# Two changes to matmul shapes in a two-layer encoder kernel: values projected like queries and keys and then transposed, and small low-rank products over all 128 rows

## The chip, the cores and the metric

One core of one Trainium2 chip runs the whole program. The metric is device time in microseconds (us) of one execution. Several executions of a kernel are timed, and their median counts. A profile is one further execution, recorded by the hardware profiler; its span runs from the first to the last instruction.

The engines are TensorE (PE for its matmuls, PEld for its weight loads), VectorE (DVE), ScalarE (ACT), GpSimdE (POOL) and SyncE (SP, which only issues DMAs here). In a matmul one operand is stationary (it is loaded into the array first, by a weight load) and the other one is moving (its columns stream through, at most 512 of them into one PSUM bank).

## What is computed

A trunk of two layers is applied to two independent sequences of 512 tokens with 1024 channels, in float32. The kernel calls them streams 0 and 1. Layer 0 mixes with windowed attention and a long convolution, layer 1 with a recurrence (RWKV-7); a convolutional feed-forward block (FFN) stands behind each. The two places that matter here:

```
# layer 0: one projection; 3 groups of 4 heads of 64, so 256 value columns a group
proj = h @ p['w_in']
qkv = proj[..., :3 * ATTN_WIDTH].reshape(B, L, 3, N_PATTERNS, ATTN_HEADS_PER_GROUP, HEAD_DIM)
...
    o = jnp.einsum('bnhqk,bnkhd->bnqhd', p / den, vw)
# layer 1: low-rank decay (w) and rate (a), inner width 64, one pair for each direction
for direction in range(2):
    w_log = -jax.nn.softplus(-(p['w0'][direction] + jnp.tanh(xw @ p['w1'][direction]) @ p['w2'][direction])) - 0.5
    ...
    a = jax.nn.sigmoid(p['a0'][direction] + (xa @ p['a1'][direction]) @ p['a2'][direction])
```

The three attention groups look at the sequence with dilation 1, 4 and 16. The kernel handles groups 1 and 2 in the order of the four residues of the token number modulo 4.

## The kernel before

Activations lie with channels on partitions and 512 tokens along the free axis, in eight tiles of 128 channels. Every float32 number is split in two parts, high and low (`h0h`, `h0l`, ...; `whi`, `wlo`), and a product is made of three matmuls: high by high, low by high, high by low. `load_w` (line 97) fetches up to 1024 weight columns with one DMA issued by ACT, makes `whi` on ACT (line 108) and `wlo` on POOL (line 112). `dense` (line 121) is the standard projection: weights stationary, 512 tokens moving, 8 x 3 = 24 matmuls into one bank of a pool of three (tile `pd`), then a copy out of it. All matmuls are recorded at line 78, transposes (a matmul by the identity, which is moving) at line 81.

**Values in layer 0** (`project`, lines 452 to 469, the branch for `hp == 0`). Attention needs the values with tokens on partitions, so here the activations are stationary and 256 weight columns move. For each of the 3 groups and 2 streams that is 96 matmuls into two `pd` banks (named `pv`), fetched as two weight loads. `perm` picks the 128 tokens of a block: for group 0 they are adjacent, for groups 1 and 2 every fourth one, so that the stationary operand is read with a stride of four values. Then ACT copies both banks into `V` (line 469). Queries and keys of the same group (line 474) are dense projections, and ACT puts their tokens into residue order while it copies them out of PSUM.

`attend` works on a pair of heads: scores on PE (`ps<-qk,qk`), mask and maximum on DVE (lines 503 and 504, or 516 and 518), exponential on ACT (line 534), transposes of the result on PE (`ps<-ident,sb`), a copy out (lines 540 and 542), the product with `V` on PE (`ps<-pt,V`). Its score tiles are called `sb` and rotate through four buffers. Its banks come from a pool of five, shared with the modulation matmuls (`ps<-adaw,sc`) that run beside stream 0.

**Wide part of layer 1** (`rw_project`, the loop that ends the function). There are 8 rounds for each stream, one for each tile of 128 output channels. A round is a dense projection of `wv`, one product with `hselt`, then for rate (`la`) and decay (`lw`) and both directions d two matmuls: `wh` with the stacked hidden tile (rows of both parts, 128 rows), and `wl` with its high part alone, which is 64 rows: 0 to 63 for d = 0 and 64 to 127 for d = 1. The sums go through a sigmoid on ACT (line 912). Two 128-row products and one 96-row product for the gate (`lg1ah`, `lg1al`, `lg1b`) and four transposes of the values follow.

Each engine works through its queue in order. The order is set in two steps: `run` and `weave` interleave the two streams and their parts by the costs that each part yields, and the tile framework's scheduler then places the instructions of each engine. While stream 1 is in layer 0, stream 0's FFN is interleaved with it; while stream 0 is in the wide part, stream 1's FFN is.

Of the kernel before, what the change touches and what calls it, by code (L numbers as in the profile page):

```python
# [8 lines left out]
F32 = mybir.dt.float32  # L9
# [8 lines left out]
L = 512  # L18
NS = 2
T = NS * L  # L20
KC = D // 128
# [30 lines left out]
class K:  # L52
# [387 lines left out]
    def attention(self, s, hs, ap, op, then, early):  # L440

        nc, a = self.nc, self.a
        xs = lambda k: hs[k]
        nd = op.tile([128, 3, 4, 2, 4], F32, name="nd")
        z = op.tile([128, 516], F32, name="places")
        nc.sync.dma_start(z, a["places"])
        nm, den = nd[:, :, :, 0], nd[:, :, :, 1]
        rel = ap.tile([128, 640], F32, name="rel")
        nc.sync.dma_start(rel, a["rel"])
        O, V, qk = {}, {}, {}  # L450

        def project(g, hp):
            if hp == 0:
                V[g] = ap.tile([128, 4, 256], F32, tag="V", bufs=2, name="V")
                pv = [self.psd.tile([128, 512], F32, tag="pd", name="pv") for _ in range(2)]
                for i in range(2):
                    wh, wl = self.load_w(a["wva"][g, :, i * 4:i * 4 + 4], 4, 256)
                    for k0 in (0, 2):
                        for b in range(4):
                            o = pv[b // 2][:, b % 2 * 256:b % 2 * 256 + 256]  # L460
                            for k in (k0, k0 + 1):
                                first, last = i + k + b % 2 == 0, i + k == 4
                                hh, hl = (self.perm(t, g, b) for t in hs[i * 4 + k])
                                self.mm(o, hh, wh[k], start=first, stop=False, skip_group_check=True)
                                self.mm(o, hl, wh[k], start=False, stop=False, skip_group_check=True)
                                self.mm(o, hh, wl[k], start=False, stop=last, skip_group_check=True)
                    yield 48 * 109
                for b in range(0, 4, 2):
                    nc.scalar.copy(V[g][:, b:b + 2], pv[b // 2].rearrange("p (b c) -> p b c", b=2))
            qk[g, hp] = []  # L470
            for i, m in enumerate((g * 2 + hp, 6 + g * 2 + hp)):
                t = ap.tile([128, L], F32, tag=f"qk{i}", bufs=2, name=f"qk{i}")
                qk[g, hp].append(t)
                yield from self.dense(a["win"][m], KC, xs, lambda ps: nc.scalar.activation(self.unperm_src(t, g), self.unperm(ps, g), AF.Copy, scale=0.125 if i == 0 else 1.0))

        parts = [(g, hp) for g in range(3) for hp in range(2)]
        yield from project(*parts[0])
        for (g, hp), nxt in zip(parts, parts[1:]):
            yield from self.weave(project(*nxt), self.attend(ap, g, hp, qk[g, hp], V[g], rel, nm, den, O, op))
        early()  # L480
        g, hp = parts[-1]
        yield from self.weave(then, self.attend(ap, g, hp, qk[g, hp], V[g], rel, nm, den, O, op))
        self.at_out = nd, z, O
# [254 lines left out]
    def rw_project(self, s, ctx):  # L738
        nc, a, side = self.nc, self.a, self.side[s]
# [150 lines left out]
        for c in range(KC):  # L890
            t = new("tv")
            yield from self.dense(a["wv"][c], KC, lambda k: xs[k], lambda ps: nc.scalar.activation(t, ps, AF.Copy, scale=0.5))
            while late:
                bonus(*late.pop())
            wh, wl = self.load_w(a["l2"][c], 6)
            r, k = get("r", c, "t1"), get("k", c, "kl")
            kk = new("nb")
            p2 = self.ps()
            q = slice(c // 2 * 32, c // 2 * 32 + 32)
            self.mm(p2, hselt[q, c % 2], rn[q], start=True, stop=True)  # L900
            nc.vector.scalar_tensor_tensor(kk, k, self.v("kk", c), p2, ALU.mult, ALU.mult)
            put("kk", c, kk)
            al = []
            for n, j in (("a", 0), ("w", 1)):
                for d in range(2):
                    ps = self.ps()
                    rows = slice(d * 64, d * 64 + 64)
                    x = hid[f"l{n}1", d]
                    self.mm(ps, wh[j * 2 + d], x, start=True, stop=False)
                    self.last = self.mm(ps, wl[j * 2 + d][rows], x[rows], start=False, stop=True)  # L910
                    lt = new("kd" if n == "a" else "po")
                    nc.scalar.activation(lt, ps, AF.Sigmoid, bias=self.v(n + "0", d * 8 + c))
                    put(f"sg{d}" if n == "w" else f"a{d}", c, lt)
                    if n == "a":
                        al.append(lt)

            ks = new("nb")
            nc.gpsimd.tensor_tensor(ks, al[0], al[1], ALU.add)
            nc.scalar.activation(ks, ks, AF.Identity, bias=ka2[:, c:c + 1], scale=self.v("ka", c))
            nc.vector.tensor_tensor(ks, ks, k, ALU.mult)  # L920
            nc.vector.scalar_tensor_tensor(k, r, self.v("rk", c), ks, ALU.mult, ALU.mult)
            yield 8 * 216
            ps = self.ps()
            self.mm3(ps, (wh[4], wl[4]), hid["lg1a"], True, False)

            nc.gpsimd.tensor_copy(wh[5][64:96], wl[5][64:96].bitcast(F32))
            self.last = self.mm(ps, wh[5][0:96], hid["lg1b", 0][0:96], start=False, stop=True)
            gt = new("po")
            nc.scalar.copy(gt, ps)
            put("g", c, gt)  # L930
            yield 4 * 216

            late.append((c, t, k))

            p2 = self.ps()
            for i in range(4):
                self.tr(p2[:, i * 128:i * 128 + 128], t[:, i * 128:i * 128 + 128], self.ident)
            p3 = p2.rearrange("p (g v) -> p g v", v=64)
            mean = o1.tile([128, 8], F32, tag="vm", bufs=2, name="vm")
            nc.vector.tensor_reduce(mean, p3, AX.X, ALU.add)  # L940
            nc.vector.tensor_scalar(mean, mean, -2.0 / 64, None, ALU.mult)
            vc = new("nb")
            nc.vector.scalar_tensor_tensor(vc.rearrange("p (g v) -> p g v", v=64), p3, 2.0, mean[:, :, None].to_broadcast([128, 8, 64]),
                                           ALU.mult, ALU.add)
            put("v", c, vc)
            yield 440
# [397 lines left out]
def layout(np, i):  # L1344
    _vec_layout()
    o = {}
# [34 lines left out]
    o["ident"] = np.eye(128, dtype=np.float32)  # L1381
    w = i["l0_w_in"]
    o["win"] = _blocks(np, w, 128)
    o["wva"] = _blocks(np, w[:, 1536:2304], 256)
    o["wout"] = _blocks(np, i["l0_w_out"], 128)
    for n in "rkvo":
        o["w" + n] = _blocks(np, i["l1_w_" + n], 128)
# [104 lines left out]
```

## Time and profile before

| | |
|---|---|
| median of 3 executions | 3535.35 us (3534.73 to 3545.4) |
| profiled execution | 3541.31 us, its span 3539.5 us |
| PE busy | 3260.7 us, 92% of the span |
| DVE, ACT, POOL busy | 48%, 44%, 45% |
| mean granted clock of TensorE | 0.952 of 2.4 GHz |

PE runs matmuls in a pipeline. The duration of one in the profile is longer than the distance to the next one's start, so costs are read here from start to start. The granted clock of a stretch is a mean of two levels, 2.4 GHz (1.00) and 1.2 GHz (0.50). Views by stretch give the busy time of each engine with the number of its instructions in brackets.

### The profile page before, as it was taken

The numbers are of one execution on the slowest core, as the hardware profiler recorded it, in microseconds if no ns is written. First come the engines' busy times: TensorE is split into PE (matmuls) and PEld (weight loads), VectorE is DVE, ScalarE is ACT, GpSimd is POOL, SyncE is SP. The second block draws the span as 40 slices with busy tenths as digits, with TensorE's granted clock in tenths as the row PEclk, the third lists the DMA queues.
The fourth block names the chain that finished last, engine by engine and source line by source line (L and its number), as shares of the span: only waits on it lengthen the run. The fifth ranks groups of instructions, "written<-read, shape, count | busy, mean of one in ns | idle before, by whom it ended". The sixth has DMA issues, their size and how long they took to land. (4 is left out here: it accounts for less than half of the span.)

```text
span 3539.5 us, 62668 instructions
## 1 busy us (share of the span) xinstructions
PE 3260.7 (92%) x24082; PEld 2336.5 (66%) x24082; DVE 1710.2 (48%) x3181; ACT 1573.0 (44%) x3137; POOL 1601.0 (45%) x1480
## 2 busy tenths in 40 slices
PE   7999999999998989999997897798999989989998
PEld 4556777778776766676665564466666666667776
DVE  5021432222356273566677658357677663442223
ACT  3123253443244445445555557445555454433332
POOL 2112443344456564454454547445455444444443
PEclk9999999999999999899998997789999999999999
DMA  7655222124243326553454441665444443443322
GB/s 251 228 203 208 87 96 81 64 89 146 66 145 129 128 86 212 183 140 95 111 127 142 118 120 47 239 234 146 104 116 121 128 105 90 131 152 93 97 89 89
DMA packets 378787, 463.26 MB, mean 131 GB/s; under 512 B 201239, under 2 KB 218903, under 8 KB 377080
## 3 DMA queue, kind: packets, MB, share of 16 engines
q1 hardware_dynamic: 302928, 247.78, 22.9%
q10 hardware_dynamic: 75560, 211.48, 18.8%
q8 instruction: 189, 3.10, 0.4%
q14 instruction: 110, 0.90, 0.1%
HBM read 378.11 MB, written 81.00 MB: 130 GB/s over the span
## 5 line engine op out<-in xcount | busy, mean ns | idle before, releaser
L112 POOL TENSOR_TENSOR wlo<-wraw,whi 128x512 fp32r<-128x512 f32 (+1 forms) x830 | 1084.7, 1311 | 1299.1 <-ACT whi L108 1134.2
L108 ACT CAST whi<-wraw 128x512 fp32r<-128x512 f32 (+1 forms) x830 | 497.6, 606 | 876.7 <-PE pd L78 713.6
L78 PE MATMUL pd<-midh,whi 128*128 128x512 f32 x704 | 290.2, 414 | 7.4 <-ACT midh L141 7.4
L78 PE MATMUL pd<-midl,whi 128*128 128x512 f32 x704 | 284.5, 404 | 1.1 <-DVE midl L144 0.5
L78 PE MATMUL pd<-midh,wlo 128*128 128x512 f32 x704 | 284.2, 404 | 0.4 <-POOL wlo L112 0.4
L328 DVE SCALAR_TENSOR_TENSOR x<-pd,ada,x 128x512 f32<-128x512 f32 x192 | 142.8, 746 | 195.1 <-PE pd L78 194.1
L78 PE MATMUL pd<-xml,whi 128*128 128x512 f32 (+1 forms) x448 | 192.5, 430 | 26.2 <-DVE xml L144 18.7
L78 PE MATMUL pd<-xmh,whi 128*128 128x512 f32 (+1 forms) x448 | 197.2, 442 | 5.3 <-ACT xmh L141 5.3
L78 PE MATMUL pd<-xmh,wlo 128*128 128x512 f32 (+1 forms) x448 | 186.9, 418 | 2.7 <-POOL wlo L112 2.6
L1233 POOL TENSOR_TENSOR Sg<-S,G 128x256 f32<-128x256 f32 x144 | 102.2, 710 | 172.0 <-DVE S L1231 161.0
L291 DVE SCALAR_TENSOR_TENSOR fa<-pd,vecs,fa 128x511 f32<-128x511 f32 x88 | 65.7, 746 | 235.1 <-ACT fa L290 235.1
L1218 ACT COPY UV<-X 32x128 f32<-32x128 f32 x512 | 131.1, 256 | 93.8 <-PE X L78 70.3
L321 DVE TENSOR_TENSOR fa<-fa,pd 128x512 f32<-128x512 f32 x88 | 60.3, 685 | 224.4 <-PE pd L78 222.3
L78 PEld LDWEIGHTS pd<-midh,whi 128*128 128x128 f32 x704 | 133.6, 190 | 42.4 <-ACT midh L141 10.2
L78 PEld LDWEIGHTS pd<-midl,whi 128*128 128x128 f32 x704 | 134.4, 191 | 34.1 <-DVE midl L144 4.8
L78 PEld LDWEIGHTS pd<-midh,wlo 128*128 128x128 f32 x704 | 134.0, 190 | 32.0 <-POOL wlo L112 1.1
L1231 DVE TENSOR_TENSOR S<-X,Sg 128x256 f32<-128x256 f32 x144 | 60.4, 420 | 187.7 <-ACT ys L1229 183.5
L78 PE MATMUL X<-UV,Am 32*32 32x64 f32 (+1 forms) x4096 | 128.3, 229 | 19.6 <-ACT UV L1218 16.9
L1148 DVE TENSOR_TENSOR W<-W,sub 128x120 f32<-128x120 f32 (+7 forms) x496 | 136.1, 274 | 11.1
L1146 DVE TENSOR_TENSOR sub<-U,W 128x120 f32<-128x120 f32 (+7 forms) x496 | 128.6, 259 | 16.0 <-DMA U<-inv 5.2
L78 PEld LDWEIGHTS X<-UV,Am 32*32 32x32 f32 (+1 forms) x4096 | 79.6, 109 | 85.5 <-ACT UV L1218 63.9
L78 PEld LDWEIGHTS pd<-xml,whi 128*128 128x128 f32 (+1 forms) x448 | 89.4, 200 | 58.5 <-DVE xml L144 30.4
(477 smaller groups left out, 7914.7 us busy)
## 6 DMA issues: line engine op xcount, KB each, us to landing
wraw<-in_up ACTq DMA_DIRECT2D x176, 512.0 KB, 3.6
adaw<-in_adaw SPq DMA_DIRECT2D x96, 512.0 KB, 6.0
wraw<-in_dn ACTq DMA_DIRECT2D x128, 256.0 KB, 2.7
wraw<-in_win ACTq DMA_DIRECT2D x36, 512.0 KB, 3.6
x<-x SPq DMA_DIRECT2D x48, 256.0 KB, 4.0
wraw<-in_dn ACTq DMA_DIRECT2D x64, 192.0 KB, 2.4
x<-res SPq DMA_DIRECT2D x32, 256.0 KB, 3.2
wraw<-in_wk ACTq DMA_DIRECT2D x16, 512.0 KB, 3.6
```

Source lines behind the costliest of these rows:

```text
L78: return self.nc.tensor.matmul(*a, **k)
L108: nc.scalar.copy(h, raw[:, o:o + w])
L112: nc.gpsimd.tensor_tensor(l, raw[:, o + p:o + p + w2], h[:, p:p + w2].bitcast(F32), ALU.subtract)
L291: nc.vector.scalar_tensor_tensor(t[:, 1:], ps[:, :L - 1], w(0), t[:, 1:], ALU.mult, ALU.add)
L321: nc.vector.tensor_tensor(act, act, ps, ALU.mult)
L328: nc.vector.scalar_tensor_tensor(x[m], ps, self.ada[l][:, 40 + m, s:s + 1], x[m], ALU.mult, ALU.add)
L1146: nc.vector.tensor_tensor(w, U4[:, :, k:, e * K + k:e * K + k + 1].to_broadcast(shape), W4[:, e:e + 1, k:k + 1, 0:k + 1].to_broadcast(shap ...
L1148: nc.vector.tensor_tensor(W4[:, :, k:, 0:k + 1], W4[:, :, k:, 0:k + 1], w, ALU.add)
L1218: nc.scalar.copy(dst, X[ur, :, uu(g)])
L1231: nc.vector.tensor_tensor(S, X[:, :, 384:512].rearrange("p d (g v) -> p d g v", g=2), self.Sg, ALU.add)
L1233: nc.gpsimd.tensor_tensor(Sg, S, self.G[:, tau, :, :, None].to_broadcast([128, 2, 2, 64]), ALU.mult)
```

## The change

For the values, each group is now two dense projections of 128 columns (48 matmuls of 512 tokens in all), each followed by a copy on ACT into a tile `vt` that takes one of the four `sb` buffers and puts the tokens into residue order, four transposes into a bank of the attention pool, and a copy on DVE into `V`. The input `wva` goes; the weights come from `win`, where they lie in tiles of 128 columns.

For decay and rate, the second matmul takes all 128 rows of `wl` and of the hidden tile, so that the product low by low is now included.

```diff
             if hp == 0:
                 V[g] = ap.tile([128, 4, 256], F32, tag="V", bufs=2, name="V")
-                pv = [self.psd.tile([128, 512], F32, tag="pd", name="pv") for _ in range(2)]
                 for i in range(2):
-                    wh, wl = self.load_w(a["wva"][g, :, i * 4:i * 4 + 4], 4, 256)
-                    for k0 in (0, 2):
-                        for b in range(4):
-                            o = pv[b // 2][:, b % 2 * 256:b % 2 * 256 + 256]
-                            for k in (k0, k0 + 1):
-                                first, last = i + k + b % 2 == 0, i + k == 4
-                                hh, hl = (self.perm(t, g, b) for t in hs[i * 4 + k])
-                                self.mm(o, hh, wh[k], start=first, stop=False, skip_group_check=True)
-                                self.mm(o, hl, wh[k], start=False, stop=False, skip_group_check=True)
-                                self.mm(o, hh, wl[k], start=False, stop=last, skip_group_check=True)
-                    yield 48 * 109
-                for b in range(0, 4, 2):
-                    nc.scalar.copy(V[g][:, b:b + 2], pv[b // 2].rearrange("p (b c) -> p b c", b=2))
+                    vt = ap.tile([128, L], F32, tag="sb", bufs=4, name="vt")
+                    yield from self.dense(a["win"][12 + g * 2 + i], KC, xs, lambda ps: nc.scalar.copy(self.unperm_src(vt, g), self.unperm(ps, g)))
+                    ps = self.ps()
+                    for b in range(4):
+                        self.tr(ps[:, b * 128:b * 128 + 128], vt[:, b * 128:b * 128 + 128], self.ident)
+                    nc.vector.tensor_copy(V[g][:, :, i * 128:i * 128 + 128], ps.rearrange("p (b c) -> p b c", b=4))
+                    yield 440
...
                     ps = self.ps()
-                    rows = slice(d * 64, d * 64 + 64)
                     x = hid[f"l{n}1", d]
                     self.mm(ps, wh[j * 2 + d], x, start=True, stop=False)
-                    self.last = self.mm(ps, wl[j * 2 + d][rows], x[rows], start=False, stop=True)
+                    self.last = self.mm(ps, wl[j * 2 + d], x, start=False, stop=True)
```

What this moves on the engines, at two places. First PE, in stream 0 of layer 0, before the change, where the values of group 1 begin (`adam` and `adaw` are modulation parameters, `pd<-h..` a dense projection):

```order
L81 MATMUL ps<-ident,adam 128x128 x4
L78 MATMUL pd<-h7h,wlo 128x512
L78 MATMUL pv<-whi,h0h 128x256
L78 MATMUL pv<-whi,h0l 128x256
L78 MATMUL pv<-wlo,h0h 128x256
L78 MATMUL pv<-whi,h1h 128x256
L78 MATMUL pv<-whi,h1l 128x256
L78 MATMUL pv<-wlo,h1h 128x256
```

Each pair of channel tiles makes four such runs of six, one for each block of tokens. The same engine and group with the change, first where one values projection (bank `pd_1020`) ends and the next one (`pd_1164`) begins:

```order
L78 MATMUL pd_1020<-h6h_425,wlo_1018 128x512
L78 MATMUL pd_1020<-h7h_432,whi_1016 128x512
L78 MATMUL pd_1020<-h7l_433,whi_1016 128x512
L78 MATMUL pd_1020<-h7h_432,wlo_1018 128x512
L78 MATMUL pd_1164<-h0h_383,whi_1156 128x512
L78 MATMUL pd_1164<-h0l_384,whi_1156 128x512
```

and then, on PE with the change, the transposes of what `pd_1020` held. Between its last matmul and them stand 132 rows; around them are the blocks of attention (`sb_1104`, `sb_1105`, `qk`, `pt`) and the modulation matmuls:

```order
L78 MATMUL ps_960<-adaw_1190,sc_81 32x512
L78 MATMUL pd_1338<-h3h_404,wlo_1332 128x512
L81 MATMUL ps_1118<-ident_70,sb_1105 128x128 x3
L78 MATMUL ps_1063<-pt_1115,V_480 64x128
L81 MATMUL ps_1142<-ident_70,vt_1009 128x128 x4
L78 MATMUL ps_960<-adaw_1190,sc_81 32x512 x2
```

So the transposes do not follow their projection directly: the scheduler has put other matmuls between. Of the twelve sets of four, the nearest have 23 or 24 rows between the last matmul of their projection and them.

Second, ACT in the same stage. Before, the two copies out of the value banks of group 1 stand near each other, ahead of the block's exponentials:

```order
L108 CAST whi<-wraw 128x512
L103 DMA wraw<-in_win 128x1024
L469 COPY V<-pv 128x512
L108 CAST whi<-wraw 128x512
L469 COPY V<-pv 128x512
L207 COPY adam<-ps 128x512
```

With the change they wait for a free `sb` buffer, and stand behind the exponentials (line 527 there) of a block and behind the copy of a later projection (`qk_1273`):

```order
L527 ACTIVATE sb,nd<-sb,nd 128x384 x2
L535 COPY pt<-ps 128x384
L467 ACTIVATE qk_1273<-pd 128x512
L457 COPY vt<-pd 128x512
L527 ACTIVATE sb,nd<-sb,nd 128x256 x2
L535 COPY pt<-ps 128x256
L517 COPY O<-ps 128x512
L527 ACTIVATE sb,nd<-sb,nd 128x256
L535 COPY pt<-ps 128x256
L527 ACTIVATE sb,nd<-sb,nd 128x256
L457 COPY vt<-pd 128x512
```

So the first value bank is emptied after a bank that was filled later, and two of the three `pd` banks are held meanwhile. In the wide part of layer 1 the sequence of instructions is the same as before, and only the operands of the second matmul of each pair differ; behind row 4400 of PE's 11236 the two orders have the same sequence.

## Rows read from the trace of the kernel before

**Rows 1.** The page, part 1: busy time and share of the span.

```profile
PE 3260.7 (92%) x24082; PEld 2336.5 (66%) x24082; DVE 1710.2 (48%) x3181; ACT 1573.0 (44%) x3137; POOL 1601.0 (45%) x1480
```

**Rows 2.** By stretch: length, busy PE, PEld, DVE, ACT, POOL, clock, DMA share, GB/s.

```profile
244.00:282.00 38.00, 37.28 (x188) 28.84 (x192) 4.22 (x10) 11.23 (x35) 5.10 (x4) 1.00 0.33 117
640.00:689.00 49.00, 47.96 (x220) 41.06 (x219) 9.52 (x16) 21.40 (x44) 13.37 (x11) 1.00 0.17 54
```

**Rows 3.** By stretch, tile `pv` alone: PE, PEld, ACT busy, clock, DMA, GB/s.

```profile
40.00:83.00 43.00, 12.72 (x96) 11.91 (x96) 1.09 (x2) 1.00 0.49 175
...
640.00:689.00 49.00, 24.04 (x96) 23.09 (x96) 1.12 (x2) 1.00 0.17 54
sum 264.00, PE 126.91 PEld 118.64 ACT 5.23; mean PE 21.15 PEld 19.77 ACT 0.87
```

**Rows 4.** Tile `pv`, weight loads: shortest, median, longest ns; first and last start.

```profile
L78 PEld LDWEIGHTS pv<-whi,h0h x24: 186/329/333, 48.2 to 645.3; 128*128 128x128 f32 x24
```

**Rows 5.** PE in order of time, stream 1, group 2: start, duration, instruction.

```profile
671.01 0.40 PE L78 MATMUL pv<-wlo,h4h 128*128 128x256 f32 x1
671.25 0.40 PE L78 MATMUL pv<-whi,h5h 128*128 128x256 f32 x1
...
672.18 0.39 PE L78 MATMUL pd<-h0h,wlo 128*128 128x512 f32 x1
672.41 0.39 PE L78 MATMUL pd<-h1h,whi 128*128 128x512 f32 x1
```

**Rows 6.** PE in order of time, one round of stream 0's wide part.

```profile
1362.70 0.50 PE L78 MATMUL ps<-la,whi 128*128 128x512 f32 x1
1363.13 0.49 PE L78 MATMUL ps<-la,wlo 64*128 64x512 f32 x1
1363.56 0.50 PE L78 MATMUL ps<-la,whi 128*128 128x512 f32 x1
...
1366.69 0.39 PE L78 MATMUL ps<-lg1ah,wlo 128*128 128x512 f32 x1
1366.92 0.39 PE L78 MATMUL ps<-lg1b,whi 96*128 96x512 f32 x1
1367.15 0.60 PE L81 MATMUL ps<-ident,tv 128*128 128x128 f32 x4
1367.50 0.47 PE L78 MATMUL pd<-xmh,whi 128*128 128x512 f32 x1
1367.82 0.39 PE L78 MATMUL pd<-xml,whi 128*128 128x512 f32 x1
```

**Rows 7.** By stretch, as in rows 2: rounds of stream 0's wide part.

```profile
1344.50:1362.30 17.80, 17.69 (x69) 12.06 (x68) 6.70 (x8) 9.41 (x15) 9.08 (x8) 1.00 0.67 229
1362.30:1380.40 18.10, 17.70 (x69) 11.94 (x68) 7.35 (x10) 9.88 (x16) 9.09 (x9) 1.00 0.65 225
1380.40:1400.80 20.40, 20.40 (x68) 14.32 (x67) 6.50 (x8) 9.49 (x15) 8.56 (x9) 0.83 0.59 199
1441.80:1462.30 20.50, 20.50 (x68) 14.32 (x67) 7.93 (x10) 9.89 (x16) 9.11 (x9) 0.83 0.53 173
```

**Rows 8.** All engines in order of time, a later round: PE's first product, DVE's `kk`.

```profile
1400.83 0.50 PE L78 MATMUL ps<-rn,hselt 32*128 32x512 f32 x1
...
1404.16 0.74 DVE L901 SCALAR_TENSOR_TENSOR nb<-kl,vecs,ps 128x512 f32<-128x512 f32 x1
```

**Rows 9.** Stream 1's wide part: one round by stretch, as in rows 2.

```profile
2246.80:2260.50 13.70, 11.95 (x44) 7.60 (x43) 7.49 (x9) 7.20 (x14) 6.65 (x6) 1.00 0.88 299
```

**Rows 10.** PE's waits in stream 1's wide part: total us, times, longest.

```profile
PE ps L78 <- DMA kl<-k: 7.5, 1, 7.5
PE ps L78 <- ACT kd L912: 6.4, 3, 3.2
```

**Rows 11.** Groups by line and shape, 40 to 700 us: busy us, mean ns, idle before.

```profile
L503 DVE SCALAR_TENSOR_TENSOR sb<-rel,ps 128x384 f32<-128x384 f32 x16 | 8.7, 550 | 17.1 <-PE ps L78 17.1
L504 DVE TENSOR_REDUCE nd<-sb 128x1 f32<-128x384 f32 x16 | 8.8, 550 | 0.4
L534 ACT ACTIVATE sb<-sb,nd 128x384 f32<-128x384 f32 x16 | 9.8, 616 | 20.7 <-DVE nd L504 20.7
```

More of the change, by code (lines that the diff above doesn't have):

```diff
@@ L1383, in layout @@
     o["win"] = _blocks(np, w, 128)
-    o["wva"] = _blocks(np, w[:, 1536:2304], 256)
     o["wout"] = _blocks(np, i["l0_w_out"], 128)
```

## The prediction

> **What bounds the kernel now.** I read the page's busy shares first, then the views by stretch for the two places that the change touches, then PE's instructions there in order of time. PE is busy for 92% of the span and no other engine for half of it [rows 1]. A share of the whole says little about one stage, so look at the stages. Where the values of group 2 are projected, PE is busy for 37.28 of 38.00 us in stream 0 and 47.96 of 49.00 us in stream 1, at the full clock, while ACT, the next one, has 11 and 21 us of work and DMA is at 0.33 and 0.17 [rows 2]. In four rounds of stream 0's wide part PE fills 17.7 to 20.5 us of stretches that are hardly longer [rows 7]. Both places are bound by what PE takes from start to start, and a saving there should shorten the program until the next thing is late. Stream 1's wide part is different: in the round shown PE is busy for 11.95 of 13.70 us with DMA at 0.88 [rows 9], and PE waits 7.5 us for a transfer and 6.4 us for ACT's sigmoids [rows 10].
>
> **The values: matmuls.** A strided weight load takes a median of 329 ns, where the shortest, of group 0, takes 186 [rows 4]. The consequence is in the starts: a values matmul of 256 columns in group 2 comes 0.24 us after the one before (671.01, 671.25), and a dense matmul of 512 columns 0.23 us (672.18, 672.41) [rows 5]. Half the columns, the same price: in groups 1 and 2 the load sets the pace, not the columns. Averaged over longer runs of these rows I take 0.235 us for both. Groups 1 and 2 of two streams are 4 x 96 = 384 matmuls, and become 4 x 48 = 192 of 512 columns: 192 x 0.235 = 45.1 us less. Group 0 is busy 12.72 us for its 96 matmuls [rows 3], the last tail and two breaks included; 48 x 0.235 = 11.3 us replace them, so 2 x 1 us at most, and I count 0.4, since stream 0's part lies in the start-up where PE waits anyway. As a check, all 576 keep PE busy for 126.91 us [rows 3], and 288 x 0.235 = 67.7: a gross 59 us, of which some 13 are pipeline tails and breaks that any order has. I keep 45.5.
>
> **The values: what is added.** Twelve sets of four transposes. Four of them stand between two starts that are 0.35 us apart (1367.15 to 1367.50), and the matmul behind takes 0.32 instead of 0.23 [rows 6]: 0.44 us a set, 12 x 0.44 = 5.3 us on PE. ACT still makes twelve copies. DVE gets twelve new copies of 512; the nearest rows are its passes of 384, 0.55 us [rows 11], so some 0.75 us each, 9 us in all, in stages where DVE is busy for 4 of 38 us [rows 2]: nothing, since PE's work covers it. The bytes fetched are the same. Does PE wait for the copies? The order shows 23 rows or more between a projection's last matmul and its transposes, over 5 us at 0.235; a copy takes 0.6. So no, as long as the scheduler's cover holds.
>
> **The values: what is late next.** With 22.6 us less PE work in stream 0's groups 1 and 2, attention's own chain has less beside it. A block with little cover shows PE a mask, a maximum and an exponential, 0.55 + 0.55 + 0.62 = 1.7 us for the first head and 1.1 more for the second [rows 11], some 3 us. The order shows one or two such places, where two score matmuls are followed by the transposes of their result with only modulation matmuls between. The bounds are 0 and all that stream 0 gains, 20 us; I take 3, near the lower one, because PE is nearly full there now [rows 2]. In stream 1 the FFN of stream 0 is the cover and doesn't run out. Values in all: 45.5 - 5.3 - 3 = **37 us** less, between 20 and 41.
>
> **Decay and rate: the rows.** In a round at the full clock, the eight matmuls that change between 128 and 64 rows start 0.43 us apart (1362.70, 1363.13, 1363.56), though each has the same 512 columns as a dense one at 0.23. The 96-row one behind a 128-row one starts after 0.23 (1366.69, 1366.92) [rows 6]. So it is the step to and from 64 rows that costs 0.20 us, and there are eight such steps in a round (seven inside the block, one to `lg1ah`). The step from the 32-row `hselt` stays. 8 x 0.20 = 1.6 us a round.
> The Trainium skill has two rules on it that don't agree. TensorEngine Tiling, Key Properties, says that changing the tiling mode drains the engine; by that the cost goes, and the trace agrees with 0.43 against 0.23. TensorE: Matmul & The Clock Gate, section on LDWEIGHTS, says that a load takes its columns' time whatever its rows; by that alone 64 and 128 rows cost the same. By the first rule the sum below stays 63, by the second it would be 37.
>
> **Decay and rate: the clock.** Rounds with the same instructions take 17.80 and 18.10 us at clock 1.00, and 20.40 and 20.50 us at 0.83 [rows 7]: in the latter the clock falls to its lower level behind the block of paced matmuls. Five of stream 0's rounds are of the second kind. If the block no longer has these steps, PE is dense through it, and I expect most of the falls to go: 5 x 2.5 = 12.5 us, and 1.5 for a shorter fall in the first round. Bounds: 0 and 14.
> A new wait stands against it. `lg1ah` needs the bank of `hselt`, which DVE frees at line 901. In one round DVE ends that at 1404.16 + 0.74 = 1404.90, and PE, having begun at 1400.83 [rows 8], would now be there at 1400.83 + 0.43 + 8 x 0.235 = 1403.1: 1.8 us of waiting, which took no time before because PE came later. What is queued behind is the rest of PE's round. I take it in half the rounds: 4 x 1.8 = 7 us. Stream 0: 8 x 1.6 + 14 - 7 = **20 us** less, between 6 (clock falls stay) and 27 (no wait).
>
> **Decay and rate, stream 1.** Three of eight rounds have a wait for ACT [rows 10] and one the wait for a transfer; there a faster PE only waits longer. The other four give 4 x 1.6 = **6 us**. Bounds: 0, since DMA is at 0.88 [rows 9], and 8 x 1.6 plus a few falls of the clock, 16.
>
> **Sum.** 37 + 20 + 6 = 63. The profiled execution took 3541.3 us, so it becomes 3478. It was 6 us above the median of the three runs (3535.35), so the median to expect is **3472 us**.
>
> **Rivals.**
> *The clock still falls* in the wide part. For it: the `kl`, `hselt` and `lg1` products and a wait remain in the block. Against: they were there in the two rounds at 1.00 too. Stream 0 gives 6, the sum is 49: 3486 us.
> *Attention runs bare in stream 0.* For it: the copies of the values hold two of three banks while they wait for an `sb` buffer behind the exponentials. Against: the modulation matmuls fill in. The values give 20, the sum is 46: 3489 us.
> *Rows don't matter*: the 0.43 us would come from something else in the block, a bank or a semaphore at each group, and stays. Against: dense groups begin without it, and the 96-row product has none. Only the values count: 3498 us. (The LDWEIGHTS rule of the Trainium skill, TensorE: Matmul & The Clock Gate, taken alone, would give this.)
> *Transposes let the clock fall.* Each of the twelve sets would be followed by a spell like that of the slow rounds, 2.5 us: 30 us back, 3502 us. Against: the values stages run at 1.00 with the transposes of attention among them [rows 2]. No row here shows a fall behind transposes alone.
> *Slower: the held banks.* A copy into `vt` waits for a buffer that attention frees; both value banks stay full, queries and keys go through one bank, and the chain closes on itself so that PE stands still for each of the twelve projections. It decides from 63 / 12 = 5.3 us a time, nearly two bare blocks of attention; at 6.5 us a time the program takes 3550 us. Against: stream 1's FFN cover in half of the cases, and an order in which PE has other rows ready each time.
>
> **How the numbers follow.** Forecast as summed 0.63, clock falls 0.13, bare attention 0.11, rows 0.05, transposes 0.03, held banks 0.03, and 0.02 for a part that saves nothing in a place I don't see. The range goes from nearly everything at its best (41 + 27 + 13 = 81: 3454) up to 3502, which takes in all rivals but the last; outside is some 0.15. A measurement of this kernel can tell 0.3%, about 11 us, from no change. All cases but the last two are faster by more than that: 0.95 faster, 0.02 the same, 0.03 slower.
>
> **What would show it.** In the profile of the changed kernel: PE's matmul count down by 288 for the values and up by 48 transposes; no weight load of 329 ns in layer 0's values; starts 0.23 us apart through the `la` and `lw` block; rounds of stream 0's wide part near 16.3 us at clock 1.00; a PE wait at `lg1ah` for DVE or ACT. Wrong would be: rounds still at 0.83 (clock rival), PE idle for tens of us between 100 and 300 us (bare attention), starts of 0.43 us that remain (rows rival), PE idle at the dense projections with ACT's `vt` as the releaser (held banks).

## The result and the profile after

The changed kernel takes 3483.36 us in the median (3481.58 to 3490.53, four executions) against 3535.04 for the kernel before beside it: a ratio of 0.9862, 95% interval 0.9821 to 0.9904. In a later job it took 3485.71 against 3530.61, ratio 0.9869 (0.9843 to 0.9895). So it is faster by 45 to 52 us. The forecast was 3472 us, 63 us less, with a range of 3454 to 3502.

The page of the changed kernel, part 1, which answers to [rows 1]. PE has 240 matmuls fewer, as counted, and 79 us less busy time in this pair of traces (64 us, 3252.3 to 3188.4, in the second pair):

```profile
PE 3181.9 (91%) x23842; PEld 2263.3 (65%) x23842; DVE 1715.5 (49%) x3193; ACT 1568.3 (45%) x3135; POOL 1598.9 (46%) x1480
```

PE in order of time in stream 1 of layer 0, group 2 (start, duration, instruction). It answers to [rows 5]: 512 columns every 0.23 us, and a set of four transposes costs what [rows 6] gave, 0.36 + 0.31 - 0.23 = 0.44 us:

```profile
659.14 0.39 PE L78 MATMUL pd<-h7h,wlo 128*128 128x512 f32 x1
659.37 0.60 PE L81 MATMUL ps<-ident,vt 128*128 128x128 f32 x4
659.73 0.48 PE L78 MATMUL pd<-h0h,whi 128*128 128x512 f32 x1
660.04 0.39 PE L78 MATMUL pd<-h0l,whi 128*128 128x512 f32 x1
660.27 0.39 PE L78 MATMUL pd<-h0h,wlo 128*128 128x512 f32 x1
```

PE in order of time in a round of stream 0's wide part, which answers to the first half of [rows 6]. The starts that were 0.43 us apart are now 0.23:

```profile
1332.42 0.39 PE L78 MATMUL ps<-la,wlo 128*128 128x512 f32 x1
1332.65 0.40 PE L78 MATMUL ps<-la,whi 128*128 128x512 f32 x1
1332.88 0.40 PE L78 MATMUL ps<-la,wlo 128*128 128x512 f32 x1
1333.12 0.39 PE L78 MATMUL ps<-lw,whi 128*128 128x512 f32 x1
1333.34 0.39 PE L78 MATMUL ps<-lw,wlo 128*128 128x512 f32 x1
```

Rounds of the same part by stretch (length, busy PE, PEld, DVE, ACT, POOL, clock, DMA share, GB/s), which answer to [rows 7]. PE has 16.4 to 16.7 us of work at the full clock, yet the four rounds shown take 17.7 to 19.5:

```profile
1313.90:1331.60 17.70, 16.42 (x68) 11.91 (x67) 6.27 (x8) 9.42 (x15) 8.56 (x8) 1.00 0.68 230
1331.60:1349.70 18.10, 16.68 (x68) 11.92 (x67) 7.34 (x10) 9.18 (x15) 8.09 (x8) 1.00 0.65 225
1349.70:1369.20 19.50, 16.48 (x69) 11.91 (x68) 6.27 (x8) 10.12 (x17) 10.53 (x10) 1.00 0.60 208
1386.80:1406.10 19.30, 16.51 (x69) 11.93 (x68) 6.27 (x8) 9.91 (x16) 10.16 (x9) 1.00 0.61 211
```

What PE waits for in these rounds (total us, times, longest). In the kernel before the first of them was 1.6 us, once (2.5 and 3.3 us in two further traces with the 64-row steps):

```profile
PE ps L81 <- ACT kd L904: 8.7, 4, 3.4
PE pd L78 <- POOL wlo L112: 3.4, 7, 0.6
PE ps L78 <- ACT kd L904: 1.8, 3, 0.8
```

Marks on the way, in us from the start of the span, with a second profiled execution of either kernel (from the experiments):

| start of | before | before, second | after | after, second |
|---|---|---|---|---|
| stream 0's output projection in layer 0 | 408.6 | 413.3 | 393.4 | 389.0 |
| statistics at the end of stream 1's first mixer | 1028.2 | 1035.4 | 990.4 | 983.1 |
| stream 0's first wide round | 1323.1 | 1330.5 | 1292.3 | 1283.6 |
| stream 0's last wide round | 1462.3 | 1462.3 | 1424.1 | 1416.5 |
| stream 1's first wide round | 2229.6 | 2217.4 | 2182.9 | 2179.5 |
| stream 1's last wide round | 2334.1 | 2322.3 | 2279.8 | 2282.0 |
| span | 3539.5 | 3524.4 | 3480.2 | 3482.1 |

Three things ask for an explanation. Nearly all of the gain stands at the end of the first mixers. Some of it is lost again before stream 0's wide part. And stream 0's wide rounds, where 20 us were forecast, give 7.4 us in the first pair (139.2 to 131.8 us for seven rounds) and nothing in the second (131.8 to 132.9). The theory after the result: the values' term is right, and in the wide part ACT has become late. The rivals: the values gain less or more than summed, by another cause than the strided load; the wide rounds are held by a bank, or the steps were never on the path.

### The profile page after: what moved, and what is told of

Same layout as the page of the kernel before. It is cut to its first block, busy times and chain, and to the rows that moved or that the text cites. A ratio compares the mean times of both kernels' runs of the same rounds, so it can differ in the third digit from the quotient of the medians.

```text
span 3480.2 us, 62175 instructions
## 1 busy us (share of the span) xinstructions
PE 3181.9 (91%) x23842; PEld 2263.3 (65%) x23842; DVE 1715.5 (49%) x3193; ACT 1568.3 (45%) x3135; POOL 1598.9 (46%) x1480
## 3 DMA queue, kind: packets, MB, share of 16 engines
q8 instruction: 187, 3.06, 0.4%
## 5 line engine op out<-in xcount | busy, mean ns | idle before, releaser
L78 PE MATMUL X<-UV,Am 32*32 32x64 f32 (+1 forms) x4096 | 127.9, 228 | 19.4 <-ACT UV L1210 16.4
```

The costliest lines, as they stand in the source:

```text
L78: return self.nc.tensor.matmul(*a, **k)
```

## Experiments

Medians are of up to 12 executions, in rounds with the kernel before on the same chip: 3529.02 us for the first four, 3526.74 for the next four, 3530.61 for the three after that, 3533.13 for the last.

**The parts alone.** The values without the rows:

```diff
+                    rows = slice(d * 64, d * 64 + 64)
-                    self.last = self.mm(ps, wl[j * 2 + d], x, start=False, stop=True)
+                    self.last = self.mm(ps, wl[j * 2 + d][rows], x[rows], start=False, stop=True)
```

> The values part alone (64-row matmuls as before). Theory: the strided weight loads were the price, worth 37 us up to the end of stream 1's layer-0 mixer (stat matmul near 990 us of the span instead of 1027), of which some 7 are lost again before the wide part, because the changed order of the second half of layer 0 makes PE wait for ACT's weight casts there. So about 30 us faster than the kernel before, near 3505, and stream 0's wide rounds still 20.5 us at clock 0.83 in about five of eight. Rival: the 7 us were a chance of one execution; then 37 faster, near 3498, and the stretch from that stat matmul to the first wide round takes 295 us as before instead of 302.

Measured: 3492.31 us, ratio 0.9902 (0.9881 to 0.9923), 36.7 us less. That is faster than either expectation. The stretch behind the first mixers takes 297.9 us, between the two. The part on the wide rounds failed: behind the first round one of six shows a clock below 1.00, at 0.91, and not five at 0.83.

The rows without the values, by the reverse edit of the kernel before:

> The 128-row part alone (values as before). Theory: PE's work in a round of stream 0's wide part falls from 17.7 (20.5 at the lower clock) to 16.5 us and the clock stays at 1.00, but rounds take 17.6 to 19.5 us, because PE now waits 1 to 3 us in each for a bank that ACT's first sigmoid frees: stream 0 some 8 us, stream 1 some 8 us, 16 to 20 us faster in all, near 3517; the stretch before the first wide round takes 295 us as before. Rival 1: the falls of the clock come from something else in the round: rounds at 0.83 remain. Rival 2: the bank wait came with the values part: rounds of 16.5 us, 28 us faster in stream 0 alone.

Measured: 3522.07 us, ratio 0.9983 (0.9964 to 1.0002): 7 us less, with 13 us less and no gain as the ends, so less than the 16 to 20 expected. The rounds take as long as the theory had them, but the rounds of 20.5 us against which it counted its gain were not there to be shortened (below). The two parts together make the whole within their intervals.

The seven full rounds of either wide part by stretch, stream 0 above stream 1: first the kernel before (second execution), then the values alone, then the rows alone, then the whole change.

```profile
1330.50:1462.30 131.80, 127.55 (x470) 86.41 (x469) 48.67 (x63) 68.70 (x111) 66.55 (x58) 0.97 0.62 212
2217.40:2322.30 104.90, 97.28 (x305) 62.26 (x305) 48.07 (x63) 50.25 (x86) 49.35 (x44) 0.85 0.78 265
```

```profile
1284.40:1417.10 132.70, 127.53 (x470) 86.05 (x469) 48.03 (x63) 68.96 (x111) 65.15 (x58) 0.97 0.61 209
2179.20:2284.00 104.80, 97.65 (x306) 62.66 (x306) 47.57 (x63) 50.36 (x86) 49.30 (x44) 0.83 0.78 266
```

```profile
1326.70:1458.20 131.50, 118.23 (x470) 85.92 (x469) 48.32 (x63) 69.04 (x112) 65.96 (x58) 0.97 0.63 212
2219.00:2318.70 99.70, 84.01 (x306) 58.67 (x306) 48.43 (x63) 49.64 (x86) 50.35 (x44) 0.88 0.80 270
```

```profile
1292.30:1424.10 131.80, 117.21 (x471) 84.68 (x470) 47.76 (x63) 68.60 (x111) 65.43 (x58) 0.99 0.62 212
2182.90:2279.80 96.90, 85.09 (x306) 59.34 (x306) 48.77 (x62) 49.41 (x85) 50.30 (x44) 0.89 0.80 278
```

With the rows PE has 9 to 10 us less to do in stream 0, and the rounds take as long as they did. In stream 1 they are 5 to 8 us shorter here. Over all traces of the experiments, those with the 64-row steps give 102.3 to 104.9 us (four, mean 104.1) and those with 128 rows and ScalarE's queue there 96.9 to 102.5 (seven, mean 99.1): 5 us in the mean, though the ends touch.

**The kernel before, once more.** No edit.

> The kernel before, unchanged, for a second profiled execution. Theory (the rounds of 20.4 to 20.5 us at a granted clock near 0.83 belong to one execution and not to the 64-row steps): stream 0's rounds show another pattern, several at 17.7 to 18.5 us and a clock of 1.00, and the profile's span is some 5 to 20 us from 3539.5. Rival (the steps cause it): four or five rounds of 20.4 us at 0.83 again.

Measured: 3526.22 us, span 3524.4. Two of its rounds, with the 64-row steps in them:

```profile
1352.40:1370.20 17.80, 17.64 (x69) 12.02 (x68) 6.71 (x8) 9.41 (x15) 9.25 (x8) 1.00 0.69 229
1388.10:1407.10 19.00, 19.00 (x68) 13.31 (x67) 6.81 (x8) 9.49 (x15) 9.15 (x9) 0.91 0.64 214
```

Five of its seven rounds show a granted clock of 1.00, none 0.83. The rounds of 20.4 us in [rows 7] belonged to that execution. They are most of the 7.4 us by which the first pair of traces differs in stream 0's rounds, and most rounds with the steps run without them.

The steps are not cleared, though. In the round of 19.00 us above the clock falls at the end of the block of steps, and PE has not waited before it: `lg1b` starts 0.42 us behind the product before it, where [rows 6] have 0.23:

```profile
1392.01 0.50 PE L78 MATMUL ps<-lg1ah,whi 128*128 128x512 f32 x1
1392.35 0.58 PE L78 MATMUL ps<-lg1al,whi 128*128 128x512 f32 x1
1392.73 0.63 PE L78 MATMUL ps<-lg1ah,wlo 128*128 128x512 f32 x1
1393.15 0.63 PE L78 MATMUL ps<-lg1b,whi 96*128 96x512 f32 x1
```

Such a fall stands in all four traces with the steps: in four of seven rounds in the first one, in one here, in one with the values alone and in two in the next experiment. It stands in none of the ten traces in which some or all of the steps are gone. There the clock falls when PE waits or has just waited, for the sigmoids in most cases. The round with the rows alone whose clock fell behind its first shows it; PE waited 2.05 us at the transposes before it:

```profile
1420.60:1440.20 19.60, 17.55 (x69) 13.24 (x68) 6.13 (x8) 9.80 (x16) 10.00 (x9) 0.91 0.60 208
```

So without the steps the falls inside the block go, and falls at waits come in their place: over the seven rounds the clock is 0.97 here and 0.97 with the rows alone. Why one execution had four falls and the others one or two is not shown.

**The stride.** In the kernel before, the stationary blocks of groups 1 and 2 are read from adjacent tokens:

```diff
-                                hh, hl = (self.perm(t, g, b) for t in hs[i * 4 + k])
+                                hh, hl = (self.perm(t, 0, b) for t in hs[i * 4 + k])
```

> The kernel before with one edit: the values of the second and third group read their stationary blocks from neighbouring tokens, as the first group's do, so these two groups' token order, and with it the attention's values, is not the reference's; the count of matmuls (1152 of 256 columns) stays. Theory: the price of the values was the strided weight load (329 ns for 128 columns, so a matmul each 0.235 us); read contiguously a matmul of 256 columns starts every 0.11 to 0.12 us and 384 of them give back about 384 x 0.115 = 44 us in each of the profile's two streams together, so the kernel comes to 3529 - 44 = 3485, as near as the whole change. Rival: the pace is set by something that every matmul pays, and the kernel stays at 3525 to 3530.

Measured: 3484.18 us, ratio 0.9884 (0.9859 to 0.9909), 42.6 us less. The weight loads of these tiles (shortest, median, longest ns) and PE in order of time in group 2, beside [rows 4] and [rows 5]:

```profile
L78 PEld LDWEIGHTS pv<-whi,h0h x24: 186/188/330, 48.3 to 612.6; 128*128 128x128 f32 x24
...
612.03 0.28 PE L78 MATMUL pv<-whi,h0h 128*128 128x256 f32 x1
612.15 0.28 PE L78 MATMUL pv<-whi,h0l 128*128 128x256 f32 x1
612.27 0.28 PE L78 MATMUL pv<-wlo,h0h 128*128 128x256 f32 x1
```

So the price of the values was the strided load: 0.12 us from start to start instead of 0.24, with the same matmuls in the same order.

**Half the steps back.** In the changed kernel only the rate keeps 128 rows:

```diff
+                    rows = slice(0, 128) if n == "a" else slice(d * 64, d * 64 + 64)
-                    self.last = self.mm(ps, wl[j * 2 + d], x, start=False, stop=True)
+                    self.last = self.mm(ps, wl[j * 2 + d][rows], x[rows], start=False, stop=True)
```

> The kernel after with half of its second part undone: the rest of the decay is read from 64 rows again, the rate's from 128, so four of the eight steps in a round are back. Theory (the rounds now wait for ScalarE's sigmoids, and what TensorE saves there only lengthens that wait): no difference that can be told, 3480 to 3488. Rival (TensorE's own time sets the round): 4 steps x 0.20 us x 16 rounds = 13 us more, 3494 to 3498.

Measured: 3486.78 us (3482.59 to 3488.2), ratio 0.9882 (0.9858 to 0.9906), not to be told from the changed kernel's. From the start of `hselt` to that of `lg1b` a round of stream 0 takes 4.66 us with all eight steps, 3.86 with these four and 3.06 with none (at the full clock, in rounds without a wait there): 0.20 us for each step. PE is busy for 124.13 us in the seven rounds, 7 us more than with the whole change, and they take 132.1. So PE's own time does not set these rounds.

**Which thing is late in the wide part?** ACT in order of time in the round at 1349.70 of the changed kernel; ACTq is its queue of issues, and in brackets stands the idle time before and what ended it:

```profile
1352.53 0.33 ACTq L103 DMA_DIRECT2D wraw<-in_l  x1
1352.91 0.62 ACT L141 CAST midh<-fa 128x512 fp32r<-128x512 f32 x1 [2.51 <-POOL wlo L112]
1353.55 1.28 ACT L904 ACT_TABLE_LOAD   x1
1354.84 1.27 ACT L904 ACTIVATE kd<-ps,vecs 128x512 f32<-128x512 f32 x2
```

and PE and POOL there:

```profile
1349.96 2.54 POOL L112 TENSOR_TENSOR wlo<-wraw,whi 128x512 fp32r<-128x512 f32 x2 [2.71 <-ACT whi L108]
...
1352.79 0.39 PE L78 MATMUL ps<-lg1b,whi 96*128 96x512 f32 x1
1355.58 0.66 PE L81 MATMUL ps<-ident,tv 128*128 128x128 f32 x4 [2.40 <-ACT kd L904]
```

PE's transposes need the bank that the first sigmoid (`kd`) frees. ACT reaches that sigmoid late: it stands at the issue of a transfer into a `wraw` buffer that POOL still reads until 1352.50, then a cast and a table load of 1.28 us come first. Two experiments part the bank from the engine. First, the transposes get a bank of the dense pool:

```diff
-            p2 = self.ps()
+            p2 = self.psd.tile([128, 512], F32, tag="pd", name="pt")
```

> The changed kernel, with the four transposes of the values in each wide round written into a bank of the dense pool (three banks) instead of the pool of five that the sigmoids empty. Theory (a bank is what PE waits for): the wait of the transposes for ACT's sigmoid, 8.7 us in stream 0, goes, stream 0's rounds fall to 16.6 to 17.5 us, and the program is 6 to 9 us faster than the changed kernel, near 3476. Rival (ACT itself is late): PE then waits the same time at the next dense projection, for the weight cast behind the sigmoids on ACT; rounds and time stay, 3483.

Measured: 3479.83 us (3472.24 to 3493.95), ratio 0.9867 (0.9842 to 0.9891). PE's waits in stream 0's rounds:

```profile
PE pd L78 <- ACT whi L108: 7.3, 5, 3.3
...
PE ps L78 <- ACT kd L904: 0.8, 1, 0.8
```

The wait at the bank goes, another one for the same engine stands in its place, and the seven rounds take 131.4 us, as the rival had it. Second, the transfers of the wide stage, with those of the FFN that run beside it, are issued from GpSimd's queue:

```diff
-        nc.scalar.dma_start(raw, src)
+        (nc.gpsimd if self.wide else nc.scalar).dma_start(raw, src)
```

> The kernel after; in the wide stage the weight tiles' transfers are issued from GpSimd's queue instead of ScalarE's. Theory: in that stage ScalarE stands still before an issue until GpSimd has read the old weights (waits of ScalarE for wlo, 7.5 + 5.4 + 3.6 + 2.5 us in stream 0's rounds), which makes the sigmoids late that TensorE waits for (8.7 us for kd there, 10.7 in stream 1). With the issue elsewhere TensorE's wait for kd falls to under 3 us in either stream, rounds of stream 0 come from 17.6 to 19.5 down to 16.8 to 17.8, and the kernel to 3466 to 3476. Rival (GpSimd's subtractions, not the queue, are late): the wait for kd turns into one for wlo, 3480 to 3490.

Measured: 3479.97 us (3472.32 to 3490.47), ratio 0.9867 (0.984 to 0.9894). The two sets of seven rounds, and PE's wait for the sigmoids in stream 0 and in stream 1:

```profile
1288.90:1412.40 123.50, 116.74 (x470) 84.48 (x469) 48.24 (x63) 70.45 (x113) 75.18 (x77) 0.99 0.66 223
2169.60:2273.80 104.20, 86.45 (x305) 60.68 (x305) 49.87 (x63) 49.68 (x86) 56.02 (x56) 0.87 0.76 258
...
PE ps L81 <- ACT kd L907: 1.0, 1, 1.0
PE ps L78 <- ACT kd L907: 1.0, 1, 1.0
...
PE ps L78 <- ACT kd L907: 10.4, 8, 3.6
```

In stream 0 the theory holds: the wait falls from 10.5 to 2.0 us and seven rounds from 131.8 to 123.5. At least 4 of these 8 us are the rows' gain, which ACT had held back: with the steps PE alone is busy for 127.5 us of the seven rounds, so no queue could have brought them to 123.5. How the rest divides is not shown, since the queue was not changed in the kernel before. In stream 1 the theory fails: the wait stays, and a new one for `tv` (6.5 us) comes to it. The seven rounds there take 104.2 us against 96.9 to 102.5, which takes back part of the gain, and the time cannot be told from the changed kernel's.

**Buffers for the projected values.** Two of their own in place of two of the four `sb`:

```diff
-                    vt = ap.tile([128, L], F32, tag="sb", bufs=4, name="vt")
+                    vt = ap.tile([128, L], F32, tag="vt", bufs=2, name="vt")
```

> The changed kernel, with two buffers of their own for the values tile, instead of a share in the four score buffers of attention. Theory (the held banks cost little): PE's waits between 80 and 420 us, 2.9 us for the exponentials and 2.6 for weight casts and parts, fall by about 3 us, and the program by 0 to 4, which is hardly measurable: 3480 to 3484. Rival (held banks cost the 5 us that stream 0 gained less than its matmul count says): 5 to 8 us faster, with stream 0's mixer ending that much earlier.

Measured: 3480.71 us (3475.08 to 3492.19), ratio 0.9867 (0.9844 to 0.9889). Stream 0's output projection starts at 387.0 us, where the two executions of the changed kernel have 393.4 and 389.0. With the same buffers in the first run under Together it starts at 392.6. So nothing that can be told from chance.

**The stretch behind the first mixers.** From the end of stream 1's first mixer to the first wide round the three traces with the values as before and the strided load take 294.7 to 295.1 us (without the stride 297.4), and the seven with the new values and the same planner's cost 297.9 to 301.9. The difference is larger than these numbers say, since nine matmuls of the stretch (2 us) now stand ahead of it. One place stands out, PE in order of time in the changed kernel:

```profile
1008.61 0.39 PE L78 MATMUL pd<-h7h,wlo 128*128 128x512 f32 x1
1014.59 0.80 PE L78 MATMUL pd<-h0h,whi 128*128 128x512 f32 x1 [5.58 <-ACT whi L108]
```

All seven traces have this wait, 5.6 us, and none of those with the values as before. In the kernel before, nine matmuls of stream 0's FFN stood between the statistics and stream 1's next projections. With the new costs that the values yield, `run` puts them elsewhere, PE starts the last matmul of the first projections at 1008.61 us, while ACT works on stream 1's norms until 1013 and casts the next weights (`whi`) behind them. A smaller cost for a set of transposes puts the nine back:

```diff
-                    yield 440
+                    yield 200
```

> The kernel after; the cost that the planner is told for a set of transposes is 200 instead of 440, nothing else. This moves work in the order: behind the statistics matmul at the end of stream 1's first mixer (990 us) stand nine matmuls of stream 0's MLP again, as in the kernel before, where the kernel after goes straight on with stream 1's projections. Theory (the wider stretch from there to the first wide round, 302 us against 295 before, is TensorE waiting 5.6 us for the weights cast behind which ScalarE's norms stand): that wait falls to about 1 us, the stretch to 295 to 298 us, the kernel to 3476 to 3482. Rival (the stretch is longer for another reason, such as the shorter values bringing stream 1 there too early for its transfers): it stays at 300 to 303 and the kernel at 3480 to 3487.

> The kernel after, unchanged, in this job, as the measure for the two beside it: 3478 to 3488, a second profile with stream 0's rounds at 17.5 to 19.8 us, a wait of 5 to 6 us for whi behind 990 us, and ScalarE's kd waited for 8 to 12 us in stream 1's rounds. If that wait and those rounds are other in this execution, they were chance and not order.

Measured: 3473.44 us (3466.95 to 3473.65), ratio 0.9838 (0.9815 to 0.986), beside 3485.71 for the changed kernel, whose second profile shows the wait again and rounds of 17.5 to 19.9 us behind the first: order, and not chance. PE's wait for `whi` in the first 70 us of the stretch, which was 5.8 us, and those 70 us, which were 75.7:

```profile
PE pd L78 <- ACT whi L108: 1.1, 1, 1.1
...
982.10:1052.10 70.00, 66.07 (x284) 51.90 (x283) 40.32 (x49) 35.44 (x61) 39.95 (x47) 1.00 0.43 139
```

The wait is explained: it is gone in all three traces with the smaller cost (this one and the two below). This first part of the stretch takes 70.0 to 72.3 us in them, against 74.2 to 75.7 in the seven, so it is worth some 4 us. The whole stretch takes 295.1, 297.2 and 299.0 in them. The medians differ by 12, with intervals that overlap; the other 8 were not traced to a place.

**Together.** First three edits at once, then the cost and GpSimd's queue, the latter for stream 0's wide stage alone (`self.wide = s == 0`):

> The kernel after with three edits together: the weights' transfers of the wide stage from GpSimd's queue, two buffers of their own for the projected values, and the planner's cost of 200 for the transposes. If the gains are separate ones: rounds of stream 0 at 16.3 to 17.5 us (8 us), 4 to 6 us in the stretch behind 990 us, 3 to 6 us in the first mixer, so 3464 to 3472 in all. If what is gained early is waited for later: 3474 to 3483.

> The kernel after with the planner's cost of 200 for the transposes and the weights' transfers from GpSimd's queue in the wide stage of stream 0 alone. With the queue changed for both streams, seven rounds of stream 0 took 123.5 and 124.5 us instead of 131.8, but those of stream 1 104.2 and 104.7 instead of 96.9 to 102.5. Theory (the queue's gain and its loss are separate): stream 0 keeps 124 us, stream 1 comes back to 97 to 102, and the kernel to 3462 to 3470, under the 3473 of the planner's cost alone. Rival (what stream 0 gains is waited for behind it, whatever stream 1's rounds do): 3471 to 3478.

Measured: 3473.57 us (ratio 0.9845, 0.9822 to 0.9867) and 3468.94 us (3463.54 to 3471.51; ratio 0.9826, 0.9809 to 0.9843). The seven rounds of either stream in the latter:

```profile
1280.10:1404.90 124.80, 116.30 (x471) 83.05 (x470) 47.76 (x63) 70.52 (x113) 74.98 (x77) 1.00 0.65 220
2162.50:2260.10 97.60, 82.97 (x305) 57.50 (x305) 49.16 (x63) 49.59 (x86) 49.70 (x44) 0.91 0.81 276
```

The first run falls between its two expectations; its rounds take 124.5 us in stream 0 and 104.7 in stream 1, which pays again. In the second stream 0 keeps its 7 us and stream 1 does not pay, as the theory had it. This is the fastest version here, though its interval overlaps that of the planner's cost alone.

## Why the prediction was right, point by point, and where it was not

**The values: right in sum, from two errors that nearly cancel.** The step "half the columns, the same price" is shown by the stride experiment: 42.6 us without touching anything else, where the working had 45.1. The transposes cost the 0.44 us that was taken. The net of 37 is what the values alone gave, 36.7. By the marks the gain was larger at first. At the end of stream 1's first mixer the seven traces with the new values and the old planner's cost stand at 982.0 to 990.4 us, 986.1 in the mean, and three with the old ones at 1028.2 to 1035.4, 1031.9 in the mean: 46 us. PE's busy time up to that mark fell by 44 us in the mean, with nine more matmuls ahead of it, where the sum had 40 (45.5 less 5.3 for the transposes). So the tails and breaks that I said any order has went in part; this follows from the sums and was not traced to rows. The 3 us for bare attention were spent (PE waits 2.9 us for the exponentials between 80 and 420 us, 0.2 before) but made up elsewhere. The next 300 us then took some 5 us back, most of it by the wait for `whi`, which the prediction didn't see; the 41 us left and the 36.7 of the values alone agree within the interval of the latter (27 to 42). That the sum came out is in part luck: I looked for what is late next inside attention, not at what a planner that goes by yielded costs does downstream.

**Decay and rate, the steps: right as PE time, wrong as time on the path.** 0.43 fell to 0.23, the block of a round from 4.66 to 3.06 us, exactly the 1.6 forecast, and PE lost 9 to 10 us of busy time in seven rounds of stream 0. The Trainium skill, TensorEngine Tiling, Key Properties, says that a change of tiling mode drains the engine, and the trace agrees with it; by the section on LDWEIGHTS of TensorE: Matmul & The Clock Gate, another page of the Trainium skill, where a load takes its columns' time whatever its rows, alone PE's time would have stayed. But the rounds did not get shorter. "Bound by what PE takes from start to start" was read from one trace in which the clock stood lower in four of seven rounds. At the full clock ACT's sigmoids follow so close behind PE that a faster PE waits for them.

**Decay and rate, the clock: right in kind, wrong in size, and the term that failed.** The 14 us counted five rounds of 20.4 us. The trace has four of them, and it was the only one with so many: the other three traces with the steps show a fall in the block in one or two rounds of seven, and two of them a mean clock of 0.97. The falls in the block did go with the steps, as forecast, but a faster PE waits for the sigmoids, and the clock falls at these waits instead. In the repeated traces nothing is left of the term (131.8 to 132.9 us). A row that shows two kinds of rounds with the same instructions is a sign that something else decides as well.

**The new wait: right in kind and near in size, wrong in place.** I put 7 us at `lg1ah`, for DVE. PE waits there 1.8 us, for ACT, and 8.7 us at the four transposes of `tv`, whose bank the first sigmoid holds. I had asked which bank the next product needs, and not which one each of the following needs.

**Stream 1's rounds: right.** 6 forecast, 5 seen in the mean. Over seven rounds PE's wait for the sigmoids went from 4.8 to 6.8 us with the steps to 10.4 to 14.1 without, as the sum had it for the rounds that wait.

**Sum.** Rows 26 forecast, 7 measured (up to 13 by its interval). The total of 63 was too high by 11 to 18; stream 0's wide part, with 20 forecast and none in the repeated traces, is more than that. The subtraction of 6 us for a long profiled execution was right in kind, but the 7.4 us by which that execution's rounds were longer are as much, and they are the clock term that I counted as a gain.

**The rivals.** "The clock still falls" (3486) gave a time near the measured one, for another reason: the falls at the end are not those in the block, and ACT's lateness holds the rounds. "Rows don't matter" (3498) falls with the starts of 0.23 us, "held banks" with the time; bare attention is there at its forecast size. "Transposes let the clock fall" has nothing for it: in the ten traces with the twelve sets no fall of the clock begins within 5 us behind one of them.

## What to carry to other kernels

A strided stationary operand is paid for in each weight load: where the moving side has few columns, exchange the operands and transpose the result. Before a saving on the busiest engine is counted, ask of every bank and buffer in the following steps how far behind its last reader is; an engine that is idle half the time can still be the next bound when its queue holds an issue that waits. A stretch whose clock differs between two executions of one kernel needs more than one trace before its clock is counted as a gain. And where costs told to a planner change, look at the whole order behind the edit, since one moved group of matmuls was worth some 4 us here.

## What the runs showed of the hardware

- A weight load of 128 columns read with a stride of four values takes 329 ns, and 188 when read contiguously; a 256-column matmul then starts every 0.24 or 0.12 us.
- A 64-row matmul among 128-row ones of the same 512 columns costs 0.20 us at each step, in and out: a block takes 4.66, 3.86 and 3.06 us with eight, four and no steps.
- In the wide rounds of stream 0 the granted clock fell inside a block of such steps or right at its end, with no idle time of PE before it, in all four traces that have the eight steps, and in none of the ten that have fewer. Without the steps it fell at PE's waits.
- The same program showed stream 0's seven wide rounds at a mean granted clock of 0.89 in one execution and 0.97 in another, 139.2 and 131.8 us. Single traces of before and after can differ by as much as a part of the change is worth.
- The gain of a queue was a matter of the stage: issuing transfers from GpSimd instead of ScalarE shortened stream 0's rounds by 8 us and did not shorten stream 1's, where DMA is at 0.8 (104.2 and 104.7 us against 96.9 to 102.5). Why not is not shown.
